# Meta tokens' key scores in four column groups, and the rotary key tile in two halves of the array

## The chip, the cores and the metric

The kernel runs on one core of a Trainium2 chip, in one launch. The metric is the device time of that launch in microseconds. Five engines work side by side: TensorE (PE in the profile: matmuls; its weight loads are the row PEld), VectorE (DVE), ScalarE (ACT), GpSimd (POOL) and SyncE (SP, which issues most DMAs). Matmul results land in PSUM; everything else works in SBUF.

## The reference, cut to what matters

Two layers work on 272 tokens (16 meta tokens ahead of 256 others) of width 1024. Each layer is a mixer block (a product with `w_in`, a convolution branch, an attention with low-rank queries and keys, gates) and then a product-key expert layer:

```python
c_q, c_kv, k_rope = z[..., o0:o1], z[..., o1:o2], z[..., o2:o3]      # z = rmsnorm(x) @ w_in
k_r = jnp.broadcast_to(k_rope[:, :, None, :], (B, L, N_HEADS, ROPE_DIM))
k = _rmsnorm(jnp.concatenate([k_nope, k_r], axis=-1), k_norm_g)       # then rope on the last 32
...
q = (hf @ wq).reshape(T, PEER_HEADS, 2, PEER_HALF)                    # hf = rmsnorm(h)
s = jnp.einsum('thpd,hpnd->thpn', q, keys)                            # 128 keys, 16 (head, half) pairs
sv, si = lax.top_k(s, PEER_TOPK)
...
a = jnp.einsum('ted,td->te', u_table[ib], xb)
out = jnp.einsum('te,ted->td', jax.nn.gelu(a) * wb, v_table[ib])
```

In the last layer the meta tokens' expert output isn't needed; in the first it is.

## The kernel before, in words

All activations stand transposed: features on the partitions, tokens along the free axis. Weights stream through a ring of four SBUF buffers of 1 MB (`wraw`, `dma_to`, L77, issued by SP as TensorE uses them up); one buffer holds two tiles of 128 output features. `ztile` (L264) makes one such tile: eight matmuls (`mm`, L55) of a 128x128 weight block against the tokens, accumulated in a PSUM tile `z`. The order of the instructions of each engine is written out by hand: the program interleaves Python generators (`stats`, `attention`, `conv2`, `layernorm`, `early`, `bg`, `gathers`) between the z tiles, and each engine takes its instructions in that order.

A layer starts with three z tiles for the low-rank queries and keys, whose squares and scaled copies go to ScalarE (L663 to L668). `stats` (L299) sums the squared inputs with a matmul by ones and starts the reciprocal root `rs` on VectorE (`rsqrt_steps`, L159). The fourth tile is the rotary one (L671): its 128 weight columns are the 32 rotary key features three times and once with the halves swapped, so that PSUM partitions 64 to 95 hold the keys and 96 to 127 the swapped ones. L673 multiplies partitions 64 to 127 by `rs` into `zkr`. `attention` (L310) then sums the squares of the low-rank tiles; after the next z tile it squares `zkr` on ScalarE (L352), sums the square with the matrix `kone` (L353) and goes on with `qhead` (L326), whose order on VectorE follows `x2` and `mq` (L318 to L321). The rotary parts of the keys are made of `zkr` at L358 to L362. The product of attention weights and values (`mix`, L491) and the sums of squares of the query heads (`qsum`, L341) write two neighbouring matmuls to different partition groups of PSUM. `seln` (L426) spreads key scales over the partitions with products of eight rows.

After the mixer and the residual, sixteen z tiles make the expert queries (L942 to L977). Tile i is copied to SBUF as `qr` (two buffers, L949) by ScalarE; after tile i the scores of tile i-1 are made (`scores`, L795): two matmuls give the scores `sc` of 256 tokens, and in layer 0 a third gives those of the meta tokens, `scm`, with 32 token columns as the weights, at partitions 32 (i mod 4) and on, so that four tiles fill one PSUM tile. VectorE takes the best 16 of each row (`top16`, L782), for `scm` once in four tiles. For tiles 12 to 15 ScalarE first copies the scores to SBUF (L808 to L815). From tile 9 on VectorE also begins the second selection (`heads`, `second`).

Then comes the activation stage: 128 tiles of `u` against 160 of the tokens (`A`), with selections and `wbuild` (its matmuls are `wp`, its one-hot inputs `ohE` and `ohA`) woven in by `bg`, while the experts of the other tokens (and, in layer 0, of the meta tokens) are fetched by indirect DMAs from GpSimd (`gb`, L1172) and worked off on VectorE (L1197, L1183). In layer 0 the meta tokens' selections are first spread to other partitions by eight DMAs of the GpSimd queue (L1057). The last stage adds the `v` tiles (`po`).

Tiles named in `MIXQ` (L34) live in the SBUF pool that is released after the scores, the others of the mixer in one that is released earlier.

Of the kernel before, what the change touches and what calls it, by code (L numbers as in the profile page):

```python
# [7 lines left out]
F32 = mybir.dt.float32  # L8
# [4 lines left out]
AF = mybir.ActivationFunctionType  # L13
# [7 lines left out]
T = 272  # L21
# [9 lines left out]

EARLY = (5, 7, 9, 11, 13)
JS = 63
MIXQ = {"xg", "sq", "uk", "qr", "rq_w", "rq_x", "rq_ym", "tkw0", "tkw1", "tkw2", "sk", "scs"}  # L34
GB = 4
LASTP = 2
RU = (1.45, 1.35)
# [10 lines left out]
def trunk_kernel(ctx: ExitStack, tc: tile.TileContext, a: dict, out: bass.AP, dbg=None, stop=None):  # L48
    nc = tc.nc
    V, S, G, PE = nc.vector, nc.scalar, nc.gpsimd, nc.tensor  # L50
# [4 lines left out]
    def mm(o, l, r, start, stop):  # L55
        PE.matmul(o, l, r, start=start, stop=stop, skip_group_check=True)  # L56
# [20 lines left out]
    def dma_to(n):  # L77
        while state["dma"] < min(n, len(ring)):
            k = ring[state["dma"]]
            r = pp.tile([128, 2, 1024], F32, name="wraw", bufs=RAW)  # L80
            if k == 0:
                first.append(r)
            else:
                nc.sync.dma_start(r, srcs[k])
            raws[k] = r
            state["dma"] += 1

    def next_w():
        k = state["use"]
        state["use"] += 1  # L90
        if k % 2 == 0:
            if k // 2 in ring:
                dma_to(ring.index(k // 2) + RAW)
            state["w"] = raws[k // 2][:, 0]
            return state["w"]
        state["w"] = raws.pop(k // 2)[:, 1]
        return state["w"]
# [92 lines left out]
    for l in range(NL):  # L190
        last = l == NL - 1
# [13 lines left out]
        class mp:  # L205

            @staticmethod
            def tile(shape, dt, name, **kw):
                return (mpa if name in MIXQ else mpb).tile(shape, dt, name=name, **kw)
        zs = ExitStack()  # L210
        zp = zs.enter_context(tc.tile_pool(name=f"z{l}", bufs=1, space=PSUM))

        def big(tag, shape, dt=F32):
            t_ = mp.tile([128, 8 * T], F32, name=tag, tag=tag)
            n = 1
            for s_ in shape:
                n *= s_
            v_ = t_[:, :n]
            if dt != F32:
                v_ = v_.bitcast(dt)  # L220
            if len(shape) == 2:
                return v_.rearrange("p (a b) -> p a b", a=shape[0])
            if len(shape) == 3:
                return v_.rearrange("p (a b c) -> p a b c", a=shape[0], b=shape[1])
            return v_

        xg, sq = big("xg", [8, T]), big("sq", [8, T])
# [36 lines left out]
        def ztile(c0, x=None):  # L264
            x = xg if x is None else x
            n = T - c0
            w_ = next_w()
            p = zp.tile([128, 512], F32, name="z", bufs=3)
            for c in range(8):
                mm(p[:, :n], w_[:, c * 128:(c + 1) * 128], x[:, c, c0:], c == 0, c == 7)  # L270
            return p[:, :n]
# [10 lines left out]
        def sums(dst, src, n):  # L282
            for c in range(n):
                mm(dst, ones, src[:, c], c == 0, c == n - 1)

        def rstd(src, n_el, n, tag):
            x = mp.tile([128, T], F32, name="rq_x")[:, :n]
            V.tensor_scalar(x, src, 1.0 / n_el, EPS, op0=OP.mult, op1=OP.add)
            y = mp.tile([128, T], F32, name="rq_y" + tag)[:, :n]
            return rsqrt(mp, x, [128, n], y)  # L290
# [372 lines left out]
        for i in range(3):  # L663
            z = zz[i] if i < 2 else ztile(0)
# [3 lines left out]
            S.activation(cq[:, i], z, AF.Copy, scale=cl[:, C_QA + i:C_QA + i + 1])  # L668
        next(sx)
        rs = vt["rs"]  # L670
        z = ztile(0)  # L671
        zkr = mp.tile([128, T], F32, name="zkr")
        V.tensor_mul(zkr[64:128], z[64:128], rs[64:128])  # L673
        att = attention()
        cvp = conv2()

# [33 lines left out]
        for i in range(16):  # L710
            z = ztile(t0)
# [37 lines left out]
        for i in range(4):  # L749
            ps = half_tile(uu)  # L750
            for f in range(2):
                c = 2 * i + f
# [4 lines left out]
        xg, sq = big("xg", [8, T]), big("sq", [8, T])  # L757
# [13 lines left out]
        keys = big("uk", [16, 128])  # L771
        nc.sync.dma_start(keys, a["keys"][l])
        scs = ExitStack()
# [8 lines left out]
        def top16(rows):  # L782

            for vals, idx, src, w in rows:
                V.max(vals[:, 0:8], src)
            for vals, idx, src, w in rows:
                V.match_replace(w, vals[:, 0:8], src, NEG)
            for vals, idx, src, w in rows:
                V.max_index(idx[:, 0:8], vals[:, 0:8], src)
            for vals, idx, src, w in rows:  # L790
                V.max(vals[:, 8:16], w)
            for vals, idx, src, w in rows:
                V.max_index(idx[:, 8:16], vals[:, 8:16], w)

        def scores(i, qT_):  # L795
            p = sp.tile([128, 512], F32, name="sc", bufs=2)
            for k, (q0, n) in enumerate(QT[:2]):
                mm(p[:, k * 128:(k + 1) * 128], qT_[:, q0:q0 + n], keys[:, i], True, True)
            if not last:

                if i % 4 == 0:
                    ohp["m"] = sp.tile([128, 512], F32, name="scm")
                q = i % 4
                mm(ohp["m"][32 * q:32 * q + 32, 0:128], qT_[:, 0:32], keys[:, i], True, True)
            ps = [p[:, 0:128], p[:, 128:256]]
            if i >= 12:
                p_, ps[0] = ps[0], mp.tile([128, 128], F32, name="scs", bufs=4)
                S.activation(ps[0], p_, AF.Copy)  # L808
                if not last and i == 15:
                    m_, ohp["m"] = ohp["m"], mp.tile([128, T], F32, name="sk", bufs=2)[:, 0:128]  # L810
                    S.activation(ohp["m"], m_[:, 0:128], AF.Copy)
            if i >= 12:

                p_, ps[1] = ps[1], wlo[:, (i - 12) * 128:(i - 11) * 128] if i < 14 else idxT.bitcast(F32)[:, i - 14]
                S.activation(ps[1], p_, AF.Copy)  # L815
            rows = []
            for k in range(2):
                w = idxT.bitcast(F32)[:, 2] if k and i >= 12 else mp.tile([128, 128], F32, name=f"tkw{k}")
                rows.append((sv[:, k, i], si[:, k, i], ps[k], w))
            if not last and i % 4 == 3:  # L820
                rows.append((svm[:, i // 4], sim[:, i // 4], ohp["m"][:, 0:128], mp.tile([128, 128], F32, name="tkw2")))
            if i >= 12:
                behind.append(rows.pop(1))
            top16(rows)
# [92 lines left out]
        ohp = {}  # L917
# [20 lines left out]

        behind = []
        pend = None  # L940
        xh = pp.tile([128, 8, T], F32, name="xh")
        for i in range(16):  # L942
            z = ztile(t0)
            if i % 3 == 1:
                k = next(ahead, None)
                if k is not None:
                    raws[k] = ep.tile([128, 2, 1024], F32, name=f"we{i}")
                    nc.sync.dma_start(raws[k], srcs[k])
            qT_ = mp.tile([128, T], F32, name="qr", bufs=2)  # L949
            S.activation(qT_[:, t0:], z, AF.Copy)  # L950
            if i == 0:
                st = sp.tile([128, 512], F32, name="st")
                sums(st[:, :TQ], sq[:, :, t0:], 1)
            if pend is not None:
                scores(i - 1, pend)
            pend = qT_
            if i == 1:
                rs = rstd(st[:, :TQ], D, TQ, "m")
            if i == 4 and not last:
                rsm = mp.tile([128, T], F32, name="sk", bufs=2)[:, 0:128]  # L960
                V.tensor_copy(rsm.rearrange("p (t h) -> p t h", h=8), rs[:, 0:16, None].to_broadcast([128, 16, 8]))
            if i == 8:

                pr_ = sp.tile([128, 512], F32, name="st")
                rsT = rpool.tile([128, 3], F32, name="rsT")
                nr = 2 if last else 3
                for k, (q0, n) in enumerate(QT[:2]):
                    PE.transpose(pr_[:, k * 128:(k + 1) * 128], rs[:, q0 - t0:q0 - t0 + n], ident)
                if not last:
                    PE.transpose(pr_[:, 256:384], rsm, ident)  # L970
            if i == 9:
                V.tensor_copy(rsT[:, 0:nr], pr_[:, 0:nr * 128].rearrange("p (k x) -> p k x", x=128)[:, :, 0])
            if i >= 9:
                next(early, None)
            if 4 <= i < 12:
                c = i - 4
                G.tensor_tensor(xh[:, c, t0:], xg[:, c, t0:], rs, op=OP.mult)  # L977
# [260 lines left out]
        for j in range(128):  # L1238
# [6 lines left out]
            w_ = next_w()  # L1245
# [28 lines left out]
        for j in range(LJ):  # L1274
            w_ = next_w()
# [130 lines left out]
```

## Time and profile before

| what | value |
|---|---|
| median of 3 runs | 1765.46 us (1762.8 to 1767.07) |
| the profiled execution's own time | 1765.53 us |
| its span, first to last instruction | 1763.8 us |
| mean granted TensorE clock | 0.996 |
| TensorE busy | 1737.4 us, 11611 matmul records |
| VectorE, ScalarE, GpSimd busy | 1107.9, 481.5, 347.7 us |
| HBM read | 556.18 MB, 316 GB/s over the span |

A row of the timeline gives the start, the time to the end of the last of the merged instructions, the engine, the line of the kernel, the operation, `out<-in`, the array's rows and columns for a matmul, the shapes and the count; in brackets stand idle time of the engine and what ended it. All matmuls by `mm` have line 56, so they are told apart by their tiles. A row of the chain of waits gives start, duration and what the chain consisted of. A row of the windows gives the stretch, its length, then the busy time (and count) of PE, PEld, DVE, ACT and POOL where they worked, the granted clock, the DMA share and GB/s. Ends of matmuls are modelled, so starts are what periods are taken from.

### The profile page before, as it was taken

To read this page: it belongs to the slowest core of one execution; us is meant where nothing else is said; L and a number is where in the kernel's file an instruction comes from. 1 tells how busy PE (TensorE), PEld (TensorE's weight loads), DVE (VectorE), ACT (ScalarE), POOL (GpSimd) and SP (SyncE) were. 2 spreads that over 40 slices of the span, in tenths; PEclk is the share of its full clock that TensorE was granted. 3 is DMA by queue.
4 is the path that set the end of the run, shared out by engine and by line. 5 is a ranking of instruction groups with operands and counts; after the bars stand their busy time and mean duration, and the time that the engine had idled before them with its cause. 6 is when DMAs were issued, how large, how long until landed. Compare 5 with 4: busy or idle time off the path is not lost.

```text
span 1763.8 us, 29499 instructions
## 1 busy us (share of the span) xinstructions
PE 1737.4 (99%) x11611; PEld 1618.5 (92%) x11611; DVE 1107.9 (63%) x2896; ACT 481.5 (27%) x1464; POOL 347.7 (20%) x392
## 2 busy tenths in 40 slices
PE   9999999998999999999999999999999999999998
PEld 7678888998999999999986888899999999999998
DVE  5687268797888644444446784597878885333332
ACT  3443103244554211000024431133355441000000
POOL 0131012212211232233200220112121112222220
PEclk9999999999999999999999999999999999999999
DMA  6223455999999999999972234669999999999995
GB/s 234 72 96 120 167 191 209 390 381 390 420 420 418 420 421 420 419 420 417 418 273 72 96 120 144 238 262 404 361 423 424 424 420 416 396 371 401 391 396 210
DMA packets 80811, 559.38 MB, mean 317 GB/s; under 512 B 9240, under 2 KB 12248, under 8 KB 13208
## 3 DMA queue, kind: packets, MB, share of 16 engines
q1 hardware_dynamic: 49488, 338.54, 48.6%
q0 software_dynamic: 30464, 218.35, 30.4%
q8 instruction: 91, 1.49, 0.3%
q10 hardware_dynamic: 720, 0.60, 0.1%
q14 instruction: 48, 0.39, 0.1%
HBM read 556.18 MB, written 1.05 MB: 316 GB/s over the span
## 4 chain that ended last, share of the span: by engine, by line
PE 84%; DMA 10%; DVE 4%; issue 1%; ACT 1%; POOL 0%; SPq 0%; DVEq 0%; POOLq 0%; ACTq 0%
PE A L56 26%; PE po L56 25%; PE z L56 24%; DMA wraw<-vn 7%; PE aps L56 4%; DMA gb<-uv,iww 2%; PE wp L56 2%; PE sc L56 1%; DVE va L1183 1%; DVE gb L1197 1%; PE xp L56 0%; DMA wraw<-w_in 0%; DVE ex L901 0%; POOL gb L1172 0%; PE scm L56 0%
## 5 line engine op out<-in xcount | busy, mean ns | idle before, releaser
L56 PE MATMUL A<-xh,wraw 128*128 128x160 f32 x3776 | 534.7, 301 | 1.2 <-ACT idxT L815 1.2
L56 PEld LDWEIGHTS A<-xh,wraw 128*128 128x128 f32 x3776 | 517.6, 191 | 1.6 <-issue 1.6
L1197 DVE SCALAR_TENSOR_TENSOR gb<-gb,xr 128x1024 f32<-128x1024 f32 x208 | 254.5, 1223 | 388.6 <-DMA gb<-uv,iww 388.5
L1172 POOL DMA_INDIRECT gb<-uv,iww x208 | 234.7, 1128 | 530.1 <-DVE va L1183 379.3
L56 PE MATMUL z<-xg,wraw 128*128 128x272 f32 (+1 forms) x1408 | 336.1, 393 | 0.6 <-DMA wraw<-w_in 0.6
L56 PEld LDWEIGHTS z<-xg,wraw 128*128 128x128 f32 x1408 | 264.9, 192 | 57.9 <-issue 8.7
L56 PE MATMUL po<-Xh,wraw 128*128 128x160 f32 x2080 | 287.6, 300 | 3.2 <-DMA wraw<-vn 2.5
L56 PEld LDWEIGHTS po<-Xh,wraw 128*128 128x128 f32 x2080 | 283.2, 190 | 6.5 <-DMA wraw<-vn 5.2
L56 PE MATMUL po<-X,wraw 128*128 128x160 f32 x2016 | 278.2, 300 | 4.4 <-DMA wraw<-vn 3.2
L56 PEld LDWEIGHTS po<-X,wraw 128*128 128x128 f32 x2016 | 274.3, 190 | 7.8 <-DMA wraw<-vn 6.2
L1183 DVE SCALAR_TENSOR_TENSOR va<-gb,am,va 128x1024 f32<-128x1024 f32 x203 | 259.9, 1280 | 2.0 <-ACT am L1208 1.8
L1207 ACT ACTIVATE am<-am 128x1 f32<-128x1 f32 x208 | 41.3, 198 | 585.6 <-DVE gb L1197 585.5
L1111 ACT ACTIVATE ohA<-ohE,wlo 128x128 f16<-128x128 f16 x320 | 105.3, 429 | 9.5 <-DVE ohE L1108 8.8
L1171 POOL COPY warm<-wraw 1x1 f32<-1x1 f32 x86 | 40.8, 475 | 313.4 <-DMA wraw<-vn 313.3
L612 POOL TENSOR_TENSOR acc<-acc,cp 128x272 f32<-128x272 f32 (+1 forms) x60 | 50.7, 845 | 244.0 <-ACT cp L611 241.6
L604 DVE SCALAR_TENSOR_TENSOR acc<-upad,cols,acc 128x272 f32<-128x272 f32 (+1 forms) x180 | 89.2, 552 | 0.2
L1208 ACT ACTIVATE am<-am,iww 128x1 f32<-128x1 f32 x208 | 61.3, 295 | 6.8
L1108 DVE TENSOR_TENSOR ohE<-ioh,idxT 128x512 f16<-128x512 f16 x160 | 60.3, 418 | 0.0
L1122 ACT ACTIVATE Xh<-wp 128x260 f32<-128x260 f32 (+18 forms) x80 | 25.0, 313 | 124.7 <-DVE Xh L1119 117.9
L56 PE MATMUL z<-xh,wraw 128*128 128x272 f32 (+1 forms) x256 | 57.3, 386 | 0.0
L56 PEld LDWEIGHTS z<-xh,wraw 128*128 128x128 f32 x256 | 48.6, 190 | 8.3
L56 PE MATMUL wp<-ohE,ohA 128*128 128x128 f16 x640 | 50.3, 219 | 4.6 <-DVE ohA L1109 4.6
(308 smaller groups left out, 1382.4 us busy)
## 6 DMA issues: line engine op xcount, KB each, us to landing
wraw<-vn SPq DMA_DIRECT2D x128, 1024.0 KB
wraw<-u SPq DMA_DIRECT2D x118, 1024.0 KB
wraw<-w_in SPq DMA_DIRECT2D x27, 1024.0 KB
wraw<-wq SPq DMA_DIRECT2D x16, 1024.0 KB
we<-u SPq DMA_DIRECT2D x10, 1024.0 KB
wraw<-w_out SPq DMA_DIRECT2D x8, 1024.0 KB
wraw<-w_mla SPq DMA_DIRECT2D x4, 1024.0 KB
wraw<-w_conv SPq DMA_DIRECT2D x4, 1024.0 KB
```

The lines of the kernel that those rows point to most:

```text
L56: PE.matmul(o, l, r, start=start, stop=stop, skip_group_check=True)
L604: V.scalar_tensor_tensor(acc[:, c, t0:], u_, weight(c, k), acc[:, c, t0:], op0=OP.mult, op1=OP.add)
L612: G.tensor_tensor(acc[:, 0, t0:], acc[:, 0, t0:], u_[:, t0:], op=OP.add)
L1108: V.tensor_tensor(E[q], ioh[:, None].to_broadcast(full), pairs(q, b), op=OP.is_equal)
L1111: S.activation(A_[1][:, t // 2, :, t % 2], E[0][:, t // 2, :, t % 2], AF.Copy, scale=wlo[:, 4 * b + t:4 * b + t + 1])
L1122: S.activation(x_, p[:, :, a:b].rearrange("p t j -> p j t"), AF.Copy, scale=1.0 / WS)
L1171: G.tensor_copy(warm[0:1], state["w"][0:1, 0:1])
L1172: G.indirect_dma_start(out=g_, out_offset=None, in_=a[f"uv{l}"], in_offset=bass.IndirectOffsetOnAxis(ap=iww[i].bitcast(I32)[:, m // 16, 0, ...
L1183: V.scalar_tensor_tensor(vac[i], r, m_, vac[i], op0=OP.mult, op1=OP.add)
L1197: V.scalar_tensor_tensor(u_, u_, 1.0, xrs[i], op0=OP.mult, op1=OP.mult, accum_out=m_)
L1207: S.activation(m_, m_, AF.Gelu_apprx_tanh)
L1208: S.activation(m_, m_, AF.Copy, scale=iww[i][:, m // 16, 1, m % 16:m % 16 + 1])
```

## The change

Two edits. In the rotary tile only the last 64 weight columns of each block are used. Even blocks accumulate in PSUM partitions 0 to 63 and odd blocks in 64 to 127. VectorE multiplies each half by `rs` (the second product goes to a buffer of the tag `sqq`) and adds the two.

In the score loop of layer 0 ScalarE makes one more copy of each tile's first 32 tokens, into `qm`, which holds four tiles and has two buffers. The four meta score matmuls of tiles i-3 to i are issued together after the full scores of tile i, for i = 3, 7, 11 and 15, one to each group of 32 partitions. The tile is added to `MIXQ`. Both layers have the first edit, only layer 0 has the second.

```diff
-MIXQ = {..., "sk", "scs"}
+MIXQ = {..., "sk", "scs", "qm"}
...
-        z = ztile(0)
+        w_, z = next_w(), zp.tile([128, 512], F32, name="z", bufs=3)[:, :T]
+        for c in range(8):
+            e = 64 * (c % 2)
+            mm(z[e:e + 64], w_[:, c * 128 + 64:(c + 1) * 128], xg[:, c], c < 2, c >= 6)
         zkr = mp.tile([128, T], F32, name="zkr")
-        V.tensor_mul(zkr[64:128], z[64:128], rs[64:128])
+        V.tensor_mul(zkr[64:128], z[0:64], rs[0:64])
+        zk2 = mp.tile([128, T], F32, name="sqq", bufs=3)
+        V.tensor_mul(zk2[64:128], z[64:128], rs[64:128])
+        V.tensor_add(zkr[64:128], zkr[64:128], zk2[64:128])
...
-                if i % 4 == 0:
+                if i % 4 == 3:
                     ohp["m"] = sp.tile([128, 512], F32, name="scm")
-                q = i % 4
-                mm(ohp["m"][32 * q:32 * q + 32, 0:128], qT_[:, 0:32], keys[:, i], True, True)
+                    for q in range(4):
+                        mm(ohp["m"][32 * q:32 * q + 32, 0:128], qms[i // 4][:, q], keys[:, i - 3 + q], True, True)
...
+        qms = {}
...
             S.activation(qT_[:, t0:], z, AF.Copy)
+            if not last:
+                if i % 4 == 0:
+                    qms[i // 4] = mp.tile([128, 4, 32], F32, name="qm", bufs=2)
+                S.activation(qms[i // 4][:, i % 4], z[:, 0:32], AF.Copy)
```

More of the change, by code (lines that the diff above doesn't have):

```diff
@@ L33 @@
 JS = 63
-MIXQ = {"xg", "sq", "uk", "qr", "rq_w", "rq_x", "rq_ym", "tkw0", "tkw1", "tkw2", "sk", "scs"}
+MIXQ = {"xg", "sq", "uk", "qr", "rq_w", "rq_x", "rq_ym", "tkw0", "tkw1", "tkw2", "sk", "scs", "qm"}
 GB = 4
```

## The prediction

> **What bounds the kernel now.** I read the page first, then TensorE's order of time around the meta scores, then the chain of waits, then the stretch around the rotary tile.
>
> ```profile
> span 1763.8 us, 29499 instructions
> PE 1737.4 (99%) x11611; PEld 1618.5 (92%) x11611; DVE 1107.9 (63%) x2896; ACT 481.5 (27%) x1464; POOL 347.7 (20%) x392
> PE 84%; DMA 10%; DVE 4%; issue 1%; ACT 1%; POOL 0%; SPq 0%; DVEq 0%; POOLq 0%; ACTq 0%
> ```
>
> TensorE (PE) is busy through 99% of the span and is 84% of the chain that ends last, so TensorE time taken away is worth something wherever TensorE is the chain, and little where the 10% DMA and 4% VectorE (DVE) are. The profiled execution took 1765.53 us for its span of 1763.8; the median of the runs shown is 1765.46, so what the sum takes from the one it takes from the other.
>
> **The meta scores as they are.** Every matmul of f32 is two records. TensorE alone, in layer 0 and then in layer 1, which has no meta scores:
>
> ```profile
> 232.82 3.94 PE L56 MATMUL z<-xg,wraw 128*128 128x272 f32 x16
> 236.59 0.61 PE L56 MATMUL sc<-uk,qr 128*128 128x128 f32 x4
> 237.13 0.41 PE L56 MATMUL scm<-uk,qr 128*32 128x128 f32 x2
> 237.47 3.93 PE L56 MATMUL z<-xg,wraw 128*128 128x272 f32 x16
> ```
> ```profile
> 1122.99 0.61 PE L56 MATMUL sc<-uk,qr 128*128 128x128 f32 x4
> 1123.43 3.62 PE L56 MATMUL z<-xg,wraw 128*128 128x256 f32 x16
> ```
>
> The layer 0 period is 237.47 - 232.82 = 4.65. A z tile that follows full-width work takes 3.67 (19.27 to 22.94 in the rotary fence below, 0.229 a record), and the four sc records take 1123.43 - 1122.99 = 0.44, or 0.109 each. So one scm matmul, of only two records (0.22), costs 4.65 - 3.67 - 0.44 = 0.54. The other 0.32 is the change to a 32-column tile and back: a gap ahead of scm, one behind it, and a late second record of the next z.
>
> **Do column tiles run at once?** The kernel has two places where neighbours go to different column tiles: the values' product (two tiles of 64 columns) and the query sums (two of 32).
>
> ```profile
> 35.34 0.64 PE L56 MATMUL aps<-sqq,strip 96*16 96x272 f32 x4
> 35.91 3.93 PE L56 MATMUL z<-xg,wraw 128*128 128x272 f32 x16
> ```
> ```profile
> 104.70 1.45 PE L56 MATMUL aps<-t,vt 128*64 128x256 f32 x12
> 106.08 0.50 PE L56 MATMUL z<-xg,wraw 128*128 128x272 f32 x1
> ```
> ```profile
> L56 PE MATMUL aps<-t,vt x2: 430/430/431, 104.7 to 104.7; 128*64 128x256 f32 x2
> ```
>
> Four query-sum records would need 4 x 0.229 = 0.92 one after another; the next z starts 0.57 behind the first. The values' twelve (eight of 256 columns at 0.216, four of 128 at 0.109) would need 2.16; they take 1.38. The third view shows two 256-column records starting together at 104.7. So two tiles do run at once at full rate. Four at once no row shows: a group of four meta scores (eight records) costs between 2 x 0.109 + 0.32 = 0.54 (all at once) and 8 x 0.109 + 0.32 = 1.19 (in turn), with 0.76 if two run at a time. I take 0.56, nearest to the rows in which nothing but the column tile keeps neighbours apart.
>
> **The rotary tile as it is.** PE, DVE and ScalarE (ACT) together in layer 0, then the answering rows of layer 1:
>
> ```profile
> 19.27 3.83 PE L56 MATMUL z<-xg,wraw 128*128 128x272 f32 x16
> 22.94 1.54 PE L56 MATMUL aps<-sqa,ones 128*128 128x272 f32 x6
> 24.32 3.83 PE L56 MATMUL z<-xg,wraw 128*128 128x272 f32 x16
> 24.98 0.45 DVE L673 TENSOR_TENSOR zkr<-z,rq_ym 64x272 f32<-64x272 f32 x1
> 25.46 0.44 DVE L318 SCALAR_TENSOR_TENSOR rq_x<-x,aps 128x272 f32<-128x272 f32 x1
> 25.46 0.43 ACT L352 ACTIVATE sqq<-zkr 32x272 f32<-32x272 f32 x1 [5.67 <-DVE zkr L673]
> 28.07 0.72 PE L56 MATMUL aps<-sqq,kone 32*128 32x272 f32 x2
> 30.75 0.50 DVE L335 SCALAR_TENSOR_TENSOR xh<-aps,cols,rope 32x272 f32<-32x272 f32 x1 [4.05 <-ACT sqq L332]
> ```
> ```profile
> 921.16 0.44 DVE L673 TENSOR_TENSOR zkr<-z,rq_ym 64x272 f32<-64x272 f32 x1
> 924.26 0.72 PE L56 MATMUL aps<-sqq,kone 32*128 32x272 f32 x2
> ```
>
> The tile's 16 records take 3.67. In two 64-column tiles they become 8 slots of 0.229 plus the tile change of 0.32, which is 2.15: 1.52 less. But zkr is gated by the rsqrt on DVE that ends just ahead of 24.98, and that doesn't move. The edit puts one multiply and one add more there, at the pitch of 25.46 - 24.98 = 0.48 each, so the square starts at 24.98 + 2 x 0.48 + 0.45 + 0.03 = 26.42 and ends 0.43 later, at 26.85; with 0.05 for the signal to TensorE, an estimate, kone can start at 26.90. TensorE would be there at 28.07 - 1.52 = 26.55: it waits 0.35, and the net gain is 1.17. In layer 1, by 921.16 and 924.26, it is 922.74 against 923.08 and again 1.18. Queued behind the two new DVE operations are x2 and mq (L318 to L321), late by 0.96, ahead of a DVE wait of 4.05 at 30.75 that hides them; without it they'd cost that 0.96. If the second product, read from other partitions than it writes, took twice as long, the net would fall to 0.7 in each layer.
>
> **The score stage.** Before the twelfth score tile (s = 11), eleven scm matmuls go (11 x 0.54 = 5.94) and two groups come (1.12): 4.82 earlier. By the end of the stage it is 16 x 0.54 - 4 x 0.56 = 6.4. Whether the end sees this is told by DVE's rows and the chain:
>
> ```profile
> 274.67 0.50 DVE L785 MAX8 sv<-sc 128x8 f32<-128x128 f32 x2 [0.54 <-PE sc L56]
> ...
> 279.32 0.50 DVE L785 MAX8 sv<-sc 128x8 f32<-128x128 f32 x2 [0.54 <-PE sc L56]
> ```
> ```profile
> 278.83 0.46 PE sc L56 x4
> ...
> 297.15 0.28 DVE si L793
> ...
> 304.50 14.37 DMA gb<-uv,iww
> ```
> ```profile
> 409.72 5.33 PE A L56 x27
> ```
>
> Up to 279.32 DVE waits for TensorE at every tile, so it moves with it. The last two waits are 0.54, just what a tile loses: DVE comes out even, and I take 0.1 off. From 279.32 to 297.15 the chain is DVE without a gap, then the gathers and DVE, and TensorE heads it again only at 409.72. So layer 0 keeps what s = 11 has gained: 1.17 + 4.82 - 0.1 = 5.9, not the 7.6 by which TensorE is ahead at the end of the stage. The remaining 1.7 turns into waiting:
>
> ```profile
> PE wp L56 <- DVE ohA L1109: 4.6, 2, 3.9
> ```
>
> This wait, in layer 0's activation stage, grows to about 6.3. Two groups at a time would make the 5.9 into 5.5, four in turn into 4.6.
>
> **New small work.** Sixteen ScalarE copies of 128x32 cost between nothing and the 0.28 of a 128x128 copy:
>
> ```profile
> L811 ACT ACTIVATE sk<-scm 128x128 f32<-128x128 f32 x1 | 0.3, 278 | 0.1
> ```
> ```profile
> 227.30:295.00 67.70, 67.22 (x324) 53.27 (x322) 53.34 (x319) 11.49 (x28) 5.78 (x8) 1.00 0.48 175
> ```
>
> ScalarE is busy 11.49 of the 67.70 in that stretch (its column follows DVE's); at most 4.5 more is hidden, and each stands behind the copy of the query, so delays nothing that the full scores need. Without that cover the last one would cost 0.28. No DMA is added or moved, nor is any queue passed.
>
> **Sum:** layer 0 5.9, layer 1 1.18 (no later DMA or DVE wait is fixed in time; each follows TensorE): 7.1. 1765.53 - 7.1 = 1758.4, and the same against the median.
>
> **What moves by itself.**
>
> ```profile
> 409.40:412.90 3.50, 3.50 (x15) 3.47 (x15) 2.98 (x7) 2.24 (x9) 0.00 (x0) 0.51 0.90 337
> 972.60:976.00 3.40, 3.40 (x9) 2.15 (x8) 3.26 (x7) 1.25 (x1) 1.83 (x3) 0.51 0.54 227
> ```
>
> In these two stretches the granted clock is 0.51: one behind the wait for ohA, one during the products of eight rows. Such a stretch costs half its length, 1.7. Work that moves may meet one more or one less; I put in none, and 1.7 to either side in the range.
>
> **Rivals.** *The clock:* the longer wait ahead of 409.72 and the moved eight-row products each meet one more half-clock stretch: 1758.4 + 3.4 = 1761.8. For it: the wait grows; against: it may as well lose one. *Records in order:* if a record can't start before the one ahead of it in the program, and a matmul's two records are neighbours there, each pair overlaps by one record only: a group takes five slots (0.86), the rotary tile nine (2.38, still covered by kone's wait), and s = 11 gains 5.94 - 1.73 = 4.21: 6.5 in all, 1759.0. The pair at 104.7 speaks against it. [...] *One tile after another:* the rotary tile keeps its 3.67 and adds 0.32 in each layer; a group costs 1.19, so s = 11 gains 5.94 - 2.38 = 3.56, and in all 2.9: 1762.6. The pair at 104.7 speaks against it. *The gain of layer 0 is absorbed:* if the gathers from 304.50 on are set by DMA traffic that doesn't move, only layer 1's 1.18 is left: 1764.3. For it: a gather takes 14.37; against: its issue follows the DVE chain, and weights are requested as TensorE uses them. *Slower, gathers crowded out:* TensorE, 1.7 further ahead, requests weight tiles that go ahead of the gathers on the chain. At the rate of
>
> ```profile
> 410.00:604.00 194.00, 194.00 (x1580) 192.55 (x1579) 160.41 (x326) 91.57 (x332) 40.04 (x39) 0.99 1.01 415
> ```
>
> a tile of 1 MB takes 2.5; from three tiles on the 7.1 is gone, and with four, one ahead of each long gather wait up to 409.72, it is 1768.4. Against it: a lead of 1.7 is well under the 4.3 that TensorE needs for one (32 records of 160 columns at 0.229 x 160/272). *Slower still, each change of column tile drains:* eight rotary matmuls of 0.46 + 0.32 take 6.2, 2.6 more in each layer, and the meta scores gain nothing: 1770.6; the twelve records in 1.38 all but exclude it.
>
> **Chances.** Forecast 0.52 (its own range 1756 to 1760.5), records in order 0.08, clock 0.10, one after another 0.10, absorbed 0.10, crowded out 0.06, draining 0.04. The range of 1755.0 to 1764.3 takes in the first five, and twice 1.7 below the forecast. About 3.5 us (0.2%) is what can be told from no change: faster by more are the first two nearly whole, most of the clock case and a little of the third: 0.70; within it 0.21; slower the last two, 0.09.
>
> **What would show it.** Right: eight scm records starting together behind sc of s = 3, 7, 11, 15, periods of 4.11 between the others; the rotary tile in about 2.15; kone waiting 0.35 for the square; DVE's first score search of s = 11 about 6 earlier; the wait for ohA longer by 1.7. Wrong: scm records in turn, a rotary tile over 3, a first gather that lands no earlier, or half-clock stretches in other number.

## The result, and the profile after

The changed kernel took a median of 1755.27 us (1754.26 to 1757.66) against 1766.26 for the kernel before: a ratio of 0.9947, with a 95% interval of 0.9930 to 0.9963, or 9.4 us less (12.4 to 6.5; the medians lie 11.0 apart). Two more comparisons of the same two kernels gave 0.9962 (0.9949 to 0.9975, 6.7 us) and 0.9940 (0.9926 to 0.9953, 10.6 us). The forecast was 7.1 less. The change is faster in all three; how much lies beyond the forecast is what the experiments are about. One execution of a kernel tried below took 2229.64 us at a granted clock of 0.753; it is left out of the times given here.

The page of the profiled execution (its own time 1755.68):

```profile
PE 1729.5 (99%) x11611; PEld 1614.6 (92%) x11611; DVE 1108.9 (63%) x2900; ACT 480.9 (27%) x1480; POOL 335.5 (19%) x392
PE 72%; DMA 10%; issue 9%; DVE 6%; POOL 2%; ACT 1%; SPq 0%; POOLq 0%; DVEq 0%; ACTq 0%
```

TensorE (PE) has as many records and 7.9 us less busy time. Its share of the chain is 72% for 84%: in this execution the chain stays with GpSimd's gathers and "issue" for longer. Its order of time around the rotary tile in layer 0, then in layer 1:

```profile
18.46 0.62 PE L56 MATMUL aps<-sq,ones 128*128 128x272 f32 x2
19.02 2.05 PE L56 MATMUL z<-xg,wraw 128*64 128x272 f32 x16
21.00 1.64 PE L56 MATMUL aps<-sqa,ones 128*128 128x272 f32 x6
22.48 3.83 PE L56 MATMUL z<-xg,wraw 128*128 128x272 f32 x16
26.50 0.72 PE L56 MATMUL aps<-sqq,kone 32*128 32x272 f32 x2 [0.19 <-ACT sqq L352]
```
```profile
908.00 0.62 PE L56 MATMUL aps<-sq,ones 128*128 128x272 f32 x2
...
916.04 0.72 PE L56 MATMUL aps<-sqq,kone 32*128 32x272 f32 x2 [0.19 <-ACT sqq L352]
```

The rotary tile takes 1.98 (19.02 to 21.00) where it took 3.67, and kone now waits for the square on ScalarE (ACT). The gap ahead of the tile and the three products behind it are each about 0.1 longer than before. From the sum of squares to the next z tile it is 22.48 - 18.46 = 4.02. In the kernel before it was 24.32 - 18.82 = 5.50, counted from this row, so 1.48 is gained:

```profile
18.82 0.62 PE L56 MATMUL aps<-sq,ones 128*128 128x272 f32 x2
```

From the sum of squares to kone it is 916.04 - 908.00 = 8.04 in layer 1 (8.04 in layer 0 too).

TensorE alone in the score stage:

```profile
231.52 0.61 PE L56 MATMUL sc<-uk,qr 128*128 128x128 f32 x4
231.97 3.83 PE L56 MATMUL z<-xg,wraw 128*128 128x272 f32 x16
235.63 0.61 PE L56 MATMUL sc<-uk,qr 128*128 128x128 f32 x4
...
239.75 0.61 PE L56 MATMUL sc<-uk,qr 128*128 128x128 f32 x4
240.28 0.43 PE L56 MATMUL scm<-uk,qm 128*32 128x128 f32 x8
240.64 3.94 PE L56 MATMUL z<-xg,wraw 128*128 128x272 f32 x16
244.41 0.61 PE L56 MATMUL sc<-uk,qr 128*128 128x128 f32 x4
```

Tiles without meta scores have a period of 4.11 (231.52 to 235.63). The one with a group of four has 4.66 (239.75 to 244.41): the group costs 0.55, as much as one meta score did alone.

The chain of waits through the stage:

```profile
266.46 0.49 DVE sv L791 x2
...
274.68 0.50 DVE sv L791 x2
...
299.87 15.22 DMA gb<-uv,iww
```

VectorE's (DVE) twelfth score search starts at 274.68 (279.32 before), the first gather is 304.50 - 299.87 = 4.63 earlier, and DVE has become the chain two tiles sooner. That is less than the 5.9 of the sum because this execution met one half-clock stretch more in layer 0, which cost 1.7 (read below); against that, its sum of squares had started 0.36 earlier (18.46 for 18.82). The granted clock in two stretches at the eight-row products and the z tile behind them, in layer 0 and in layer 1:

```profile
75.40:82.30 6.90, 6.90 (x16) 4.74 (x16) 4.65 (x10) 1.28 (x1) 1.88 (x3) 0.51 0.28 116
966.30:969.80 3.50, 3.50 (x10) 2.79 (x9) 2.70 (x7) 0.00 (x0) 0.06 (x1) 0.51 0.00 0
```

Before, the half clock lasted 3.4 in the first place and 6.8 in the second; now it is the other way round. What one such stretch of 3.4 costs is read in layer 0, from the z tile ahead of these products to the product behind the z tile that follows them. With two of them, in the changed kernel, it is 84.03 - 69.20 = 14.83; with one, in the kernel before, 83.92 - 70.79 = 13.13; the difference is 1.7. The z tile ahead in the changed kernel, then in the kernel before:

```profile
69.20 3.94 PE L56 MATMUL z<-xg,wraw 128*128 128x272 f32 x16
```
```profile
70.79 3.93 PE L56 MATMUL z<-xg,wraw 128*128 128x272 f32 x16
```

### The profile page after: what moved, and what is told of

It is laid out like the page before. It is cut to its first block, busy times and chain, and to the rows that moved or that the text cites. A ratio compares the mean times of both kernels' runs of the same rounds, so it can differ in the third digit from the quotient of the medians.

```text
span 1753.9 us, 29518 instructions
## 1 busy us (share of the span) xinstructions
PE 1729.5 (99%) x11611; PEld 1614.6 (92%) x11611; DVE 1108.9 (63%) x2900; ACT 480.9 (27%) x1480; POOL 335.5 (19%) x392
## 4 chain that ended last, share of the span: by engine, by line
PE 72%; DMA 10%; issue 9%; DVE 6%; POOL 2%; ACT 1%; SPq 0%; POOLq 0%; DVEq 0%; ACTq 0%
PE po L56 27%; PE z L56 22%; PE A L56 16%; DMA wraw<-vn 6%; DMA gb<-uv,iww 4%; PE aps L56 4%; POOL gb L1183 2%; PE wp L56 1%; DVE va L1194 1%; DVE gb L1208 1%; PE sc L56 1%; PE xp L56 0%; DMA wraw<-w_in 0%; DVE rq_w L172 0%; DVE ex L907 0%
## 5 line engine op out<-in xcount | busy, mean ns | idle before, releaser
L56 PE MATMUL z<-xg,wraw 128*128 128x272 f32 (+2 forms) x1408 | 331.6, 393 | 0.2 <-DMA wraw<-w_in 0.2
L56 PEld LDWEIGHTS z<-xg,wraw 128*128 128x128 f32 (+1 forms) x1408 | 261.9, 191 | 55.0 <-issue 8.0
L1182 POOL COPY warm<-wraw 1x1 f32<-1x1 f32 x86 | 32.6, 379 | 319.7 <-DMA wraw<-vn 319.7
```

The source lines that it names most:

```text
L1182: G.tensor_copy(warm[0:1], state["w"][0:1, 0:1])
```

## The experiments

**Each edit alone.** The kernel before with only the rotary edit, and with only the meta scores' edit.

```diff
-        z = ztile(0)
+        w_, z = next_w(), zp.tile([128, 512], F32, name="z", bufs=3)[:, :T]
+        for c in range(8):
+            e = 64 * (c % 2)
+            mm(z[e:e + 64], w_[:, c * 128 + 64:(c + 1) * 128], xg[:, c], c < 2, c >= 6)
...
```

> The rotary edit alone, the meta scores as before. If the terms of the sum simply add: the rotary tile takes about 1.98 (as with both edits) in each layer, kone waits about 0.3 for the square, 1.2 to 1.3 gained per layer, so 2.5 us less than before, a half-clock stretch of 1.7 more or fewer aside. Rival, that the part of the gain beyond the sum (some 3 us) is set off by this edit: 5 us or more less, and the wait of TensorE for ohA in layer 0's activation stage, 3.9 before, gone here as it is with both edits. Rival, one tile after the other: 0.7 us slower.

```diff
-                mm(ohp["m"][32 * q:32 * q + 32, 0:128], qT_[:, 0:32], keys[:, i], True, True)
+                    for q in range(4):
+                        mm(ohp["m"][32 * q:32 * q + 32, 0:128], qms[i // 4][:, q], keys[:, i - 3 + q], True, True)
...
```

> The meta-score edit alone, the rotary tile as before. If the terms add: a group costs 0.45 beyond the full scores' own time or less than 0.6, the twelfth score tile starts 4.8 earlier and the end comes about 4.7 us earlier, a half-clock stretch of 1.7 more or fewer aside. Rival, that the part beyond the sum comes from this edit (TensorE meeting the gathers otherwise): 8 us or more less, and the wait for ohA under 1. Rival, that DVE holds the stage: the first gather lands no earlier and the gain stays under 2 us.

The rotary edit gave 0.9991 (0.9980 to 1.0002): 1.6 us less, between 3.5 less and 0.4 more, which holds the 2.5 of the sum and not 5. The meta scores gave 0.9968 (0.9957 to 0.9979): 5.6 less (7.6 to 3.7), which holds 4.7 and not 8. Together 7.2. TensorE's waits in layer 0 from the score stage on, for the rotary edit alone and for the meta scores alone (total, times, longest):

```profile
PE wp L56 <- DVE ohA L1115: 6.4, 2, 4.6
```
```profile
PE wp L56 <- DVE ohA L1114: 3.5, 2, 2.3
```

So neither edit takes this wait away; with both it was 0.6 in the first profile. Both rivals, which had it gone or under 1, fall.

**Do column tiles run at once?** Both edits, and four more matmuls behind each group, into one column tile or spread over four; nothing reads their results.

```diff
+                    for q in range(4):
+                        mm(ohp["m"][0:32, 128:256], qms[i // 4][:, q], keys[:, i - 3 + q], True, True)
```

> Both edits, and behind each group of four meta scores four more matmuls of the same size, all into the first column tile and into columns that nothing reads. If column tiles run at once because each has its own work to do, four in one tile have to go in turn: a group is longer by 8 records x 0.109 = 0.87. If the groups are short only because the change of tile is paid once, both this and the spread one add 0.87.

```diff
+                    for q in range(4):
+                        mm(ohp["m"][32 * q:32 * q + 32, 128:256], qms[i // 4][:, q], keys[:, i - 3 + q], True, True)
```

> The same four more matmuls behind each group, spread over the four column tiles. All four at once: a group is longer by 2 x 0.109 = 0.22. Two at a time: 0.44. One after another: 0.87, as with all in one tile.

TensorE behind the full scores of the same tile group, all extras in one column tile:

```profile
240.26 1.28 PE L56 MATMUL scm<-uk,qm 128*32 128x128 f32 x16
241.47 0.73 PE L56 MATMUL z<-xg,wraw 128*128 128x272 f32 x2
```

and spread over four:

```profile
236.88 0.64 PE L56 MATMUL scm<-uk,qm 128*32 128x128 f32 x16
237.45 0.73 PE L56 MATMUL z<-xg,wraw 128*128 128x272 f32 x2
```

From the first meta score to the next z tile it is 1.21 and 0.57, against 0.36 (240.28 to 240.64) without extras: 0.85 and 0.21 more, where 0.87 and 0.22 stood for tiles that work at once. So the four column tiles ran here at the full rate of each, eight more records in 0.21 where two in a row take 0.22; it isn't only that the change of tile is paid once. These were single executions, of 1759.49 and 1752.37; the first met three half-clock stretches more, so at 1.7 each 5.1 of the 7.1 between them, and no reading is taken from the two times.

**Does the order of the two halves matter?** Both edits, with the even blocks first.

```diff
-        for c in range(8):
+        for c in (0, 2, 4, 6, 1, 3, 5, 7):
             e = 64 * (c % 2)
```

> Both edits, but the four even blocks of the rotary tile first and then the four odd ones. If each column tile takes its matmuls as they come, whatever stands between, the tile still takes about 2; if a matmul can only overlap neighbours in the program, only the turn from even to odd overlaps and it takes 3.5 to 3.9, with kone 1.5 later than in the changed kernel in each layer.

```profile
18.65 3.02 PE L56 MATMUL z<-xg,wraw 128*64 128x272 f32 x16
21.60 1.64 PE L56 MATMUL aps<-sqa,ones 128*128 128x272 f32 x6
```

The tile takes 2.95 and kone comes 0.70 later than in the changed kernel (8.74 behind the sum of squares, in both layers), between the two expectations, so both fell. In the trace the records form two sequences at a pitch of 0.229: eight from 18.65, the last at 20.30, and eight from 19.62. A record doesn't name its half; the sequence that ends last, with the signal that the tile is done, is taken for the odd one, which is last in the program. The odd half begins when five even records have started and three are still to start. Read so, the odd half started ahead of three even records that are earlier in the program, and no further ahead; the 2.95 is 0.72 under the 3.67 of sixteen records in turn, about three records of 0.229. What sets that distance was not tried.

**What is the draw of one execution?** "Draw" stands for what differs between executions of one and the same kernel. Both kernels again, unchanged, and the changed one a third time.

> The kernel before once more. If its wait of 3.9 for ohA and its four half-clock stretches belong to its order of work, they return; if they are one run's draw, the wait lies between 0 and 4 and the stretches are two to five.

> The changed kernel once more. If the half-clock stretches fall where the clock's own windows happen to lie, their number and places differ from the first profile (two in layer 0's eight-row products, one in layer 1's), and the span with them by steps of 1.7; if they follow from the order of the work alone, they are the same. The same holds for TensorE's wait for ohA in layer 0 (0.6 in the first profile): steady if the change removed it, between 0 and 4 if it depends on when a gather lands.

> The changed kernel, more rounds, beside the next. If the sum of 7.1 is its worth and the first comparison's larger gain was draws of half-clock stretches and of one gather's landing, the ratio to the kernel before is 0.996 (7 us). If the larger gain belongs to the change, it is 0.994 to 0.995.

The same view of waits as above, of the kernel before, then of the changed one again and a third time:

```profile
PE wp L56 <- DVE ohA L1109: 0.9, 2, 0.7
```
```profile
PE wp L56 <- DVE ohA L1120: 5.2, 2, 3.2
```
```profile
PE wp L56 <- DVE ohA L1120: 4.7, 2, 4.1
```

Together with the first profiles the wait is 4.6 and 0.9 before, and 0.6, 5.2 and 4.7 after. Half-clock stretches of 3.4 at the eight-row products (layer 0, layer 1) are 1 and 2, then 1 and 0 before; 2 and 1, 2 and 0, 1 and 0 after. Neither belongs to the change; both belong to an execution, with 1.7 us to a stretch and up to 4.6 between two waits of one kernel. The third comparison's 0.9940 went with the larger gain, against the expectation of 0.996, so times alone didn't settle it.

**Taking the draw away.** The products by seln over 128 rows, 120 of them zeros, in the changed kernel (twice, then once more beside the kernel before with the same edit).

```diff
-        seln = mp.tile([8, 8, 128], F32, name="seln")
+        seln = mp.tile([128, 8, 128], F32, name="seln")
...
-        V.tensor_copy(seln, ident[0:8, 0:8, None].to_broadcast([8, 8, 128]))
+        V.tensor_copy(seln, ident[:, 0:8, None].to_broadcast([128, 8, 128]))
...
-            rk = mp.tile([16, T], F32, name="mq")[0:8]
-            S.activation(rk, pk[0:8, :T], AF.Copy)
+            rk = mp.tile([128, T], F32, name="mq")
+            G.memset(rk, 1.0)
+            S.activation(rk[0:8], pk[0:8, :T], AF.Copy)
```

> The changed kernel with the products by seln made over all 128 rows (120 of them zeros) where they had 8; one memset of 128x272 on GpSimd more. If the half clock behind these products comes from how few rows they use, it is gone in both layers, 1.7 for each stretch, so 3.4 to 6.8 us less than the changed kernel. If it comes from their spacing or from waits on VectorE, the stretches stay and the time is the same within 1.7.

> The changed kernel with the products by seln over 128 rows, once more. If their 8 rows bring the half clock on, no half-clock stretch stands behind these products in either layer in this profile too, and the time is 3 to 4 us under the changed kernel's (about two stretches of 1.7 in a mean run). If the first profile merely met none, one to three return and the times agree within 1.5.

> The kernel before with the products by seln over 128 rows. Without the half-clock draws behind these products this and the next are compared with less scatter. If their 8 rows are the cause: no half-clock stretch behind them, 3 to 4 us less than the kernel before. If not: the same time.

> The changed kernel with the same products over 128 rows. If the change is worth the sum of its terms, it stands 7.1 us under the one above; if the larger gain of two of the three comparisons belongs to the change and not to the draws, 9 us or more.

The medians of the changed kernel with this edit were 1751.35 and 1752.10, 7.7 and 3.7 below the changed kernel beside it (6.0 and 3.6 between the means). The kernel before with this edit: 0.9960 (0.9945 to 0.9975), 7.1 less, about twice the 3 to 4 expected. TensorE around these products, first in the changed kernel, then in it with 128 rows:

```profile
73.07 5.32 PE L56 MATMUL aps<-mq,seln 8*128 8x272 f32 x16
78.31 5.88 PE L56 MATMUL z<-xg,wraw 128*128 128x272 f32 x16
84.03 0.41 PE L56 MATMUL aps<-kh,xh 98*128 98x144 f32 x2
```
```profile
73.40 3.83 PE L56 MATMUL aps<-mq,seln 128*128 128x272 f32 x16
77.07 3.83 PE L56 MATMUL z<-xg,wraw 128*128 128x272 f32 x16
80.74 0.64 PE L56 MATMUL aps<-kh,xh 98*128 98x144 f32 x3
```

From the first product by seln to the product behind the z tile, 10.96 became 7.34. The granted clock of the second kernel is 1.00 there in both layers:

```profile
73.40:81.00 7.60, 7.60 (x36) 6.36 (x35) 6.74 (x16) 2.95 (x5) 2.40 (x3) 1.00 0.42 140
961.00:969.00 8.00, 8.00 (x39) 6.86 (x38) 6.91 (x17) 2.92 (x5) 2.34 (x3) 1.00 0.36 131
```

In the ten profiles of kernels with eight rows there are 21 such stretches, 2.1 in a mean one; in the four with 128 rows there is none. At 1.7 each that is 3.6. The one profile of eight rows that met no such stretch in either layer (four column tiles, extras spread) shows what else they cost:

```profile
69.13 3.94 PE L56 MATMUL z<-xg,wraw 128*128 128x272 f32 x16
...
80.62 0.64 PE L56 MATMUL aps<-kh,xh 98*128 98x144 f32 x3
```

From the z tile ahead it is 11.49, and 11.11 with 128 rows (69.63 to 80.74): 0.4 more in layer 0 at the full clock. With as much taken for layer 1, an estimate from this, 4.4 of the 3.7 to 7.7 is accounted for; what the rest is was not tried.

The clock records also tell which places are hit. In all 14 profiles every change of the clock lies on a grid of 3.41 us, whose place differs between executions. In the first profile of the changed kernel half clock lasts from 75.45 to 82.28, 389.48 to 392.89, 601.10 to 604.52 and 966.33 to 969.74, starts that lie 92, 154 and 261 steps of 3.413 behind the first. The busy time of the eight-row products alone in steps of this grid, first in layer 0 of the changed kernel, then in layer 1 of its second profile:

```profile
72.04:75.45 3.41, 2.38 (x10) 1.00 0.33 79
75.45:78.87 3.42, 2.93 (x7) 0.50 0.54 228
```
```profile
963.03:966.44 3.41, 2.17 (x10) 1.00 0.26 53
966.44:969.86 3.42, 1.76 (x8) 1.00 0.60 254
```

In the 14 places where these products filled 2.37 or more of a step, the next step had half the clock. In the four where no step held more than 2.11 of them, none had. Of the two places in between, the one at 2.16 had it and the one at 2.17 (above) hadn't. A second half-clock step followed in the six places where they went on for 1.27 or more of the first, and not where it was 0.61 or less. So in 18 of the 20 places this draw went with where the grid lay in the execution. The stretches' 3.4 and 6.8 are one and two steps of it; products that follow each other without a gap, but of few rows, brought it on, and behind the same products over 128 rows there was none.

With this draw gone the change gives a median of 1759.13 without it and 1751.88 with it, side by side: 7.25 apart. Between the means it is 6.1, within about 2.6 (an estimate from the scatter of these executions), and by the two ratios to the kernel before 4.9; one of the six executions, at 1757.98, makes most of that difference. The sum had said 7.1, the rival 9 or more: the rival falls, and the sum is met no more closely than this.

## Why the prediction was right

**The direction and the steps** held. *The rotary tile:* 2.15 was said with the change of tile in it. The 1.48 gained up to the next z tile leaves 3.67 - 1.48 = 2.19, so the change costs 0.36, close to the 0.32 taken over from scm; the 1.98 alone leaves out the gap ahead and the late record behind. The prediction had the second of VectorE's products as the one that reads other partitions than it writes. It is the first, and it took 0.43 (L676) for the other's 0.44, so the doubled price didn't come. *kone's wait for the square* is there as the new bound, with 0.19 of idle time (0.27 by starts: kone comes 4.02 behind the start of the z tile ahead, 3.75 before) where 0.35 was said; the square ended at 26.46 and kone started at 26.50, so the signal took 0.04 where 0.05 was estimated; from the sum of squares to kone it is 8.04 in layer 1 against 9.26 before (915.00, first row below, to 924.26): 1.22 for the 1.18. *The group of four* at 0.55 for 0.56, the rival of records in order (0.86) and that of one tile after another (1.19) are both out; the extras confirm it. *The twelfth score search:* counted from the first product behind the half-clock stretches (the second row below, 83.92, and 84.03 above, so 0.1 late) it gained 4.64 + 0.1 = 4.74, for 4.82 - 0.1. *DVE comes out even* was right to the point that its waits are gone behind the tile at 266.46. The two rows of the kernel before that these counts rest on, TensorE alone:

```profile
915.00 0.62 PE L56 MATMUL aps<-sq,ones 128*128 128x272 f32 x2
```
```profile
83.92 1.57 PE L56 MATMUL aps<-kh,xh 98*128 98x144 f32 x8
```

**Two steps were off.** At the end of the score stage TensorE was to be 6.4 ahead by the meta scores and is 5.9:

```profile
286.93 1.42 PE L56 MATMUL sc<-uk,qr 128*128 128x128 f32 x8
288.28 0.43 PE L56 MATMUL scm<-uk,qm 128*32 128x128 f32 x8
289.34 0.92 PE L56 MATMUL A<-xh,wraw 128*128 128x160 f32 x5 [0.64 <-ACT idxT L821]
```

The same end in the kernel before:

```profile
292.61 0.61 PE L56 MATMUL sc<-uk,qr 128*128 128x128 f32 x4
...
295.11 0.38 PE L56 MATMUL A<-xh,wraw 128*128 128x160 f32 x1 [0.58 <-ACT idxT L815]
```

The last full scores wait for ScalarE's copy of their query, and the activation stage for ScalarE's last copy, as they did before (0.64 now, 0.58 then). So from the full scores of tile 14 to the first A it is 2.41 for 2.50: the last two single meta scores had stood in time that is waited through anyway. It cost nothing, since DVE was the chain by then. The second is the step that turned TensorE's lead into a longer wait for ohA: the wait went to 0.6 in the first profile and came out between 0.6 and 6.4 over the runs. What moved it in one execution, the landing of one gather, is read from the chain and was not tried; over the profiles no lasting loss or gain of this stage can be told.

**The size.** The intervals of the first comparison (6.5 to 12.4) and of the second (4.4 to 9.0) hold 7.1; that of the third (8.3 to 13.1) doesn't. The edits alone add to 7.2, within about 2.7, and without the eight-row draws it is 4.9 to 7.25. So the sum of terms stands, though not to the tenth. The median of 1755.27 lies under the forecast's own range (1756 to 1760.5) and just inside the whole one from 1755.0; how far it lies under 1758.4 is in part the luck of the executions compared. The granted clock of every execution of the second and third comparison is on record; with the time that it says was lost to half clock taken off, the differences between the means, 7.2 and 10.1, become 6.4 and 8.9. So half-clock stretches made about 1 us of the third comparison's excess. The draw of the wait may have made more of it, which is argued, not shown.

## What to carry to other kernels

Here matmuls of 64 output rows (the rotary tile, 1.98 where it took 3.67) and of 32 (four meta scores in 0.55, where one took 0.54) shared TensorE when neighbours in the program went to different column tiles. Issue such ones alternating (1.98, and 2.95 with the halves in turn), and bundle them, because going to narrow tiles and back cost about the same however many there were between (0.32 for one meta score, 0.33 for four, 0.36 for the rotary tile). A gain on TensorE is worth what the engine that becomes the chain next lets through: count it at that handover (here 4.74, at VectorE's twelfth score search), not at the end of the stage (here 5.9). And where two profiles differ by steps of 1.7 us, look at the granted clock before explaining it.

## What was not expected of the hardware

Products of 8 rows, back to back for 3.9 us at the full clock (962.05 to 965.91 in layer 1 of the changed kernel), brought on half the clock in 15 of 20 places (ten profiles, two layers), and the place of the 3.41 us grid told which in 18. The same products over 128 rows, mostly zeros, never did in 8 places, though in three of them they filled 3.16 to 3.41 of a step, and with the change they made the kernel with the lowest medians here: 1751.35 to 1752.10, or 0.9921 (0.9908 to 0.9935) of the kernel before in its closest comparison. And with the halves in turn a column tile's work started three records ahead of its turn in the program, the tile taking 2.95 and not 3.67.
